# One level of Strassen's product in a decoder layer's up projection, with up and down as separate stages

## The chip, the cores and the metric

The kernel runs on one core of one Trainium2 chip. The metric is the device time of one execution in microseconds (us); the kernel before was run three times and the median counts. The engines are TensorE (PE; PEld is its weight load), VectorE (DVE), ScalarE (ACT), GpSimd (POOL) and SyncE (SP, which here only issues DMAs).

## The reference, cut to what matters

One layer of a hybrid decoder: an input projection, a group of attention heads beside a group of gated DeltaNet heads, an output projection, then an MLP, a gated per-layer embedding and a last norm. Sequence length and model width are 1024, the hidden width of the MLP is 4096, everything is float32. The change lies in the MLP:

```python
m = rmsnorm(h, norm_mlp[i])
h = h + jnp.square(jax.nn.relu(m @ w_up[i])) @ w_down[i]
```

## The kernel before

The residual stream is kept transposed, 128 channels by 1024 tokens in each of 8 tiles, in two halves of 512 tokens; `hT(hb, j)` (L989) is tile j of half hb. Every large product is made in three passes: `split` (L210) cuts a float32 operand into a high part (a cast on ScalarE, L211) and a low part (a subtraction on VectorE or GpSimd, L212), and `mm3` (L224) issues high x high, high x low and low x high into one PSUM bank. All matmuls go through one helper, so in the profile they have the line L95.

The weights come in blocks of 128 rows by 512 columns: `wunit` (L214) and `wunit2` (L270) load a raw block through SP into the pool `wraw` (two buffers) and split it into a buffer of `wsp` (four buffers), or, for the down projection, of `wdn` (six buffers).

The MLP: `norm_M` (L1189) scales the residual by the norm's gain and cuts it into high and low parts, 8 tiles for each half of the tokens, into M (the first half) and R1 (the second). `rows_M` (L1197) sums the squares over the channels and makes the row of reciprocal roots `rB`, by which results are multiplied after the product. Then a loop over 8 blocks of 512 hidden columns (L1257): two times (mp) an up unit of 256 columns, 8 contraction tiles x 2 column tiles x 2 halves x 3 passes = 96 matmuls into four banks; then `relu2` (L1239) evicts each bank on VectorE (maximum with zero, times `rB`, L1244), squares it on ScalarE (L1245) and splits it into `aT`. The 512 new hidden rows are used at once: the down product of the block (2 x 2 groups of 4 banks, 4 contraction tiles, 192 matmuls) is added to the residual on VectorE (L1295). Up units and down groups use four banks each in turn.

After the MLP comes the gate stage (from L1298): 16 gate weight blocks are split into M and R1, and for each of 8 token tiles the residual is transposed, multiplied and written out.

The order of the instructions on each engine is not that of the text: the framework's scheduler plans it with a simulated clock from the dependencies, the buffers that are free and the priority (the order of the text, or an earlier one under `ahead(mark)`, L266). On the chip each engine then follows its planned list.

Of the kernel before, what the change touches and what calls it, by code (L numbers as in the profile page):

```python
# [18 lines left out]
P = 128  # L19
# [92 lines left out]
def hybrid_block(ctx, tc, t, out):  # L112
# [111 lines left out]
    def mm3(o, lh, rh, first, last):  # L224
        for i, (a, b) in enumerate(PASSES):
            T.matmul(o, lh(a), rh(b), start=first and i == 0, stop=last and i == 2)
# [951 lines left out]

    px = ExitStack()
    mt0p = px.enter_context(tc.tile_pool(name="mt0p", bufs=1))  # L1180
    atp2 = px.enter_context(tc.tile_pool(name="atp2", bufs=1))
    wdn = px.enter_context(tc.tile_pool(name="wdn", bufs=6))
    M = [mt0p.tile([P, 8192], F32R, tag="M0", name="M0"), R1]
    aT = atp2.tile([P, 2, 4, S], F32R, tag="aT", name="aT")
    rB = [rsb[1]]

    FIRST = (4, 5, 0, 1, 2, 3, 6, 7)

    def norm_M(hb):  # L1189

        for j in FIRST:
            h, g = hT(hb, j), gmlp[:, j:j + 1]
            A.activation(uview(M[hb], 0, j), h, AF.Copy, scale=g)
            V.scalar_tensor_tensor(uview(M[hb], 1, j), h, g, uview(M[hb], 0, j).bitcast(F32),
                                   op0=ALU.mult, op1=ALU.subtract)

    def rows_M(hb):  # L1197
        for j in range(KT):
            x = cvp.tile([P, HB], F32, tag="cv", name=nm("sq")) if j else rB[hb]
            A.activation(x, hT(hb, j), AF.Square)  # L1200
            if j:
                V.tensor_tensor(rB[hb], rB[hb], x, op=ALU.add)
        yield
# [5 lines left out]
        yield  # L1209
        b, dg = bank(ps["w"]), row_bc(r, aT[:, :, 3, HB:])  # L1210
        yield
# [8 lines left out]
    psum(px, y=4, w=1)  # L1220
    zr, hn = part("Z"), part("AT0")
    rB.append(zr[:, 0:HB])
    with ahead(mark):
        norm_M(0)
        for _ in rows_M(0):
            pass
    norm_M(1)

# [10 lines left out]
    def relu2(b, m, hb):  # L1239
        if m % 2:  # L1240
            r = cvp.tile([P, 512], F32, tag="cv", name=nm("r"))
        else:
            r = zr[:, D + 512 * hb:D + 512 * hb + 512]
        V.scalar_tensor_tensor(r, b, 0.0, rB[hb], op0=ALU.max, op1=ALU.mult)  # L1244
        A.activation(r, r, AF.Square)  # L1245
        hi = aT[:, 0, m, hb * HB:(hb + 1) * HB]
        lo = aT[:, 1, m, hb * HB:(hb + 1) * HB]
        split(hi, lo, r, G)

    def late(bs):  # L1250

        yield from rows_M(1)
        for m in range(2):
            relu2(bs[m], m, 1)
        yield

    for c in range(FF // 512):  # L1257
        for mp in range(2):
            bs = quad() if c else banks(("wyyy", "gggy")[mp])
            order = range(KT // 2) if c + mp else [k // 2 for k in FIRST[::2]]  # L1260
            for i, k2 in enumerate(order):
                w = wunit2(t["w_up"], k2, c * 512 + mp * 256, G if k2 % 2 else V)
                if not c and mp:
                    for _ in range((0, 1, 2, 3).count(i)):
                        next(steps, None)
                for kk in range(2):
                    kt = k2 * 2 + kk
                    for hb in range(2):
                        for m in range(2):
                            o = kk * 256 + m * P  # L1270
                            mm3(bs[hb * 2 + m], lambda a: w[:, a, o:o + P],
                                lambda b: uview(M[hb], b, kt), i + kk == 0, i * 2 + kk == KT - 1)
            if c + mp == 0:
                rows_M(1)
            for hb in range(2):
                if c + mp == 0 and hb:
                    steps = late(bs[2:])
                    continue
                for m in range(2):
                    relu2(bs[hb * 2 + m], mp * 2 + m, hb)  # L1280
        for nh in range(2):
            wd = []
            for hb in range(2):
                bs = quad()
                for kt in range(4):
                    if hb == 0:
                        wd.append(wunit(t["w_down"][c * 512 + kt * P:c * 512 + (kt + 1) * P,
                                                    nh * 512:(nh + 1) * 512],
                                        sp=wdn, lo_eng=G if kt % 2 else V))
                    for m in range(4):  # L1290
                        mm3(bs[m], lambda a: wd[kt][:, a, m * P:(m + 1) * P],
                            lambda b: aT[:, b, kt, hb * HB:(hb + 1) * HB], kt == 0, kt == 3)
# [6 lines left out]
    for kt in range(KT):  # L1299
        for nh in range(2):  # L1300
            i = kt * 2 + nh
            o = (i % 8) * 1024
            m = M[i // 8]
# [12 lines left out]
    aTf = aT.rearrange("p b m s -> p (b m s)")  # L1316

    for tt in range(NT):

        nT = aTf[:, (tt % 4) * 2048:(tt % 4 + 1) * 2048].rearrange("p (b k s) -> p b k s", b=2, k=KT)  # L1320
# [115 lines left out]
```

## Time and profile before

| | |
|---|---|
| median of 3 runs | 1414.74 us (1413.67 to 1417.92) |
| profiled execution | 1413.97 us, span 1412.2 us |
| mean granted TensorE clock | 0.987 |
| the MLP's matmuls | from 579.0 to 1285.0 us of the span |
| instructions | 20118 |
| DMA traffic | 90.31 MB |

The span reaches from the first to the last instruction. A group of instructions is shown with its busy time and the mean of one; an engine's idle time is put down to what ended it. Matmuls overlap each other, so the spacing of their starts is their price, not the length of one.

### The profile page before, as it was taken

How to read it: one execution, taken by the hardware profiler on the slowest of the kernel's cores; microseconds unless marked ns; L12 is line 12 of the kernel's file. 1: busy time of each engine (PE TensorE's matmuls, PEld its weight loads, DVE VectorE, ACT ScalarE, POOL GpSimd, SP SyncE). 2: the span in 40 equal slices, each digit the busy share in tenths (PEclk: the TensorE clock that was granted, in tenths of full speed). 3: DMA queues.
4: the chain of work that ended last, by engine and by line, in shares of the span. 5: the costliest groups of instructions: out<-in, count | busy, mean ns of one | idle time of the engine just before them, and what ended most of it. 6: DMA issues, size and time to landing. Idle time of an engine off the chain costs nothing.

```text
span 1412.2 us, 20118 instructions
## 1 busy us (share of the span) xinstructions
PE 1369.5 (97%) x7760; PEld 1160.4 (82%) x7760; DVE 702.5 (50%) x1446; ACT 493.9 (35%) x1013; POOL 490.5 (35%) x492
## 2 busy tenths in 40 slices
PE   9989999899997999999999999999999999999997
PEld 7788778788887899888888888888888888888886
DVE  6776967998579965443121231212313223255333
ACT  7455465444343344351220312203122031344222
POOL 6673636531555343241320413204132041321222
PEclk9999999999999999999999999999999999999999
DMA  6312222223123222211210112101121011241101
GB/s 217 90 46 77 60 53 65 65 68 76 44 84 116 63 87 75 76 52 45 67 45 30 53 46 68 45 30 52 45 68 45 30 53 45 81 135 38 46 30 45
DMA packets 81200, 90.31 MB, mean 64 GB/s; under 512 B 15600, under 2 KB 63264, under 8 KB 81104
## 3 DMA queue, kind: packets, MB, share of 16 engines
q1 hardware_dynamic: 78208, 83.27, 19.9%
q10 hardware_dynamic: 2544, 4.99, 1.1%
q8 instruction: 61, 1.00, 0.3%
q0 software_dynamic: 352, 0.76, 0.2%
q14 instruction: 35, 0.29, 0.1%
HBM read 83.73 MB, written 5.26 MB: 63 GB/s over the span
## 4 chain that ended last, share of the span: by engine, by line
PE 78%; DVE 13%; DMA 3%; issue 2%; ACT 2%; POOL 1%; SPq 1%; POOLq 0%; DVEq 0%; ACTq 0%
PE bk L95 76%; DVE tp L771 2%; PE bk L99 2%; DVE cv L404 2%; DVE XS L772 1%; DMA AT<-in_xT 1%; DVE w L212 1%; POOL rsb L350 1%; DVE s L541 1%; DVE s L550 1%; DMA raw<-in_w_in 1%; DVE et L772 1%; DVE H L404 0%; ACT w L211 0%; DVE ka L741 0%
## 5 line engine op out<-in xcount | busy, mean ns | idle before, releaser
L95 PE MATMUL bk<-R,w 128*128 128x256 f32 (+1 forms) x1920 | 359.6, 334 | 4.4 <-DVE H L1014 3.0
L212 POOL TENSOR_TENSOR w<-raw,w 128x512 fp32r<-128x512 f32 x140 | 188.4, 1348 | 486.2 <-ACT w L211 382.6
L95 PE MATMUL bk<-aT,w 128*128 128x512 f32 x1536 | 349.8, 389 | 0.0
L211 ACT CAST w<-raw 128x512 fp32r<-128x512 f32 (+1 forms) x244 | 151.2, 620 | 554.5 <-PE bk L95 370.1
L95 PEld LDWEIGHTS bk<-aT,w 128*128 128x128 f32 x1536 | 288.3, 188 | 60.3
L95 PEld LDWEIGHTS bk<-R,w 128*128 128x128 f32 x1920 | 290.9, 192 | 46.9 <-issue 6.9
L212 DVE TENSOR_TENSOR w<-raw,w 128x512 fp32r<-128x512 f32 (+1 forms) x104 | 78.7, 757 | 248.4 <-ACT w L211 248.3
L95 PE MATMUL bk<-M,w 128*128 128x512 f32 x768 | 198.9, 394 | 0.0
L95 PEld LDWEIGHTS bk<-M,w 128*128 128x128 f32 x768 | 144.3, 188 | 34.5
L1295 DVE TENSOR_TENSOR H<-bk,H 128x512 f32<-128x512 f32 x96 | 64.8, 689 | 103.7 <-PE bk L95 103.7
L212 POOL TENSOR_TENSOR aT<-Z,aT 128x512 fp32r<-128x512 f32 x32 | 41.5, 1298 | 137.2 <-ACT aT L211 137.2
L95 PE MATMUL bk<-U,w 128*128 128x512 f32 (+1 forms) x384 | 76.3, 345 | 1.6 <-ACT ba L464 1.1
L95 PEld LDWEIGHTS bk<-U,w 128*128 128x128 f32 x384 | 58.4, 188 | 18.0 <-issue 7.3
L95 PE MATMUL bk<-w,R 128*128 128x256 f32 (+1 forms) x480 | 70.3, 298 | 0.1
L95 PE MATMUL bk<-w,U 128*128 128x256 f32 (+2 forms) x384 | 65.9, 326 | 3.4 <-ACT AT L470 1.6
L95 PEld LDWEIGHTS bk<-w,R 128*128 128x128 f32 x480 | 63.7, 200 | 2.5 <-issue 1.9
L95 PEld LDWEIGHTS bk<-w,U 128*128 128x128 f32 x384 | 57.2, 198 | 10.0 <-ACT AT L470 1.8
L1295 DVE TENSOR_TENSOR AT<-bk,AT 128x512 f32<-128x512 f32 x32 | 21.8, 690 | 57.0 <-PE bk L95 57.0
L547 ACT ACTIVATE s<-s,mx 128x257 f32<-128x257 f32 (+1 forms) x64 | 31.2, 490 | 50.8 <-DVE mx L545 46.4
L95 PE MATMUL bk<-R,aT 128*128 128x512 f32 (+1 forms) x204 | 47.8, 383 | 0.0
L95 PE MATMUL bk<-M,aT 128*128 128x512 f32 (+1 forms) x204 | 47.0, 378 | 0.0
L212 POOL TENSOR_TENSOR aT<-r,aT 128x512 fp32r<-128x512 f32 x32 | 45.2, 1413 | 0.2 <-ACT aT L211 0.2
(338 smaller groups left out, 1780.8 us busy)
## 6 DMA issues: line engine op xcount, KB each, us to landing
raw<-in_w_in SPq DMA_DIRECT2D x72, 256.0 KB, 2.8
raw<-in_w_up SPq DMA_DIRECT2D x64, 256.0 KB, 2.7
raw<-in_w_down SPq DMA_DIRECT2D x64, 256.0 KB, 2.9
raw<-in_w_o SPq DMA_DIRECT2D x32, 256.0 KB, 3.0
rawg<-in_w_gate SPq DMA_DIRECT2D x16, 256.0 KB, 2.9
AT<-in_xT SPq DMA_DIRECT2D x14, 256.0 KB, 3.9
out<-AT SPq DMA_DIRECT2D x7, 512.0 KB, 2.6
H<-in_xT ACTq DMA_DIRECT2D x3, 1024.0 KB, 5.1
```

The lines of the kernel that those rows point to most:

```text
L95: self.tc.nc.tensor.matmul(o, lh, rh, **k)
L99: self.tc.nc.tensor.transpose(o, x, i)
L211: A.copy(hi, src)
L212: lo_eng.tensor_tensor(lo, src, hi.bitcast(F32), op=ALU.subtract)
L350: eng.tensor_tensor(acc, acc, xr, op=ALU.add)
L404: V.scalar_tensor_tensor(cv if i < 3 else x[:, 3:], x[:, i:i + HB], cw[:, j, i:i + 1], cv, op0=ALU.mult, op1=ALU.add)
L541: V.tensor_tensor_reduce(out=s[:, i, lo:256], in0=b[:, i, lo:256], in1=amask[:, lo:256], scale=1.0, scalar=NEG, op0=ALU.add, op1=ALU.max, ...
L547: A.activation(s[:, i, lo:257], s[:, i, lo:257], AF.Exp, bias=mx[:, i:i + 1], accum_out=sm[:, i:i + 1])
L550: V.tensor_tensor(s[:, :, lo:256], s[:, :, lo:256], bc(sm, 2, 256 - lo), op=ALU.mult)
L771: V.tensor_tensor(tp, bc(LS[:, j, j + 1:32], 1, m), bc(X3[:, 0:m, j], 2, n), op=ALU.mult)
L772: V.tensor_tensor(X3[:, 0:m, j + 1:32], X3[:, 0:m, j + 1:32], tp, op=ALU.subtract)
L1295: V.tensor_tensor(h, bs[m], h, op=ALU.add)
```

## The change

The up projection is done in 16 units of 256 hidden columns. In each the weights (1024 x 256) and the activations are seen as 2 x 2 blocks: the contraction's 8 tiles are cut into even and odd ones, the hidden columns into two times 128, the tokens into two halves. Strassen's product, in Winograd's form, makes the four result blocks from 7 products instead of 8. The sums of activation blocks are made once, before the loop (`first_half`, `second_half`), and kept as seven operands X[1] to X[7], each split into high and low; X1, X2, X6 and X7 lie in the eight buffers of a new pool `mt`, X5 and X3 in R1, X4 in two parts that the output projection uses before. The sums of weight blocks are made on VectorE for each unit. `product` makes one of the seven products: 4 contraction tiles x 3 passes; products 2, 7 and 3 are accumulated onto the banks of products 1, 6 and 5, after these have been read. A unit uses four banks, the next unit the other four. The weights of products 4 and 3 share one buffer (`we`). The four result blocks are evicted (`put`), squared, and written to DRAM (`AD`, 16 tiles of 1 MB) through SP.

The first two units run product 1 of both, product 2 of both, and then the rest. After all 16 units a new loop makes the down projection: per block it loads four tiles of 128 x 1024 from `AD`, splits them into buffers of `mt`, and multiplies as before. The first block comes in half tiles through `wraw`, and its first four weights use `wsp` instead of `wdn`. `wdn` has five buffers and is opened when the up stage's pool `uw` is closed. The gate weights and token tiles of the last stage use R1 and `mt`.

```diff
-    def mm3(o, lh, rh, first, last):
+    def mm3(o, lh, rh, first, last, **k):
...
+    mt = px.enter_context(tc.tile_pool(name="mt", bufs=8))
+    ux = ExitStack()
+    uw = ux.enter_context(tc.tile_pool(name="uw", bufs=1))
+    AD = [dram.tile([P, 2048], F32, tag=f"AD{n}", name=f"AD{n}") for n in range(16)]
...
+    def tmp(i, n=HB):
+        p, tag, w = ((cvp, "cv", HB), (wraw, "raw", WN), (uw, "o", HB))[i]
+        return p.tile([P, w], F32, tag=tag, name=nm("t"), bufs=3 if i == 2 else None)[:, :n]
...
+    def first_half(i):
+
+        for p, j in ((1, 2 * i), (2, 2 * i + 1)):
+            h, g, (hi, lo) = hT(0, j), gmlp[:, j:j + 1], (cols(x, i) for x in X[p])
+            A.activation(hi, h, AF.Copy, scale=g)
+            V.scalar_tensor_tensor(lo, h, g, hi.bitcast(F32), op0=ALU.mult, op1=ALU.subtract)
+
+    def second_half(i):
+
+        j, k = 2 * i, 2 * i + 1
+        gj, gk = gmlp[:, j:j + 1], gmlp[:, k:k + 1]
+        t1, t2, t3, t4 = tmp(0), tmp(1), tmp(2), tmp(2)
+        G.tensor_tensor(t1, hT(1, j), hT(0, j), op=ALU.subtract)
+        A.activation(t1, t1, AF.Copy, scale=gj)
+        A.activation(t3, hT(1, j), AF.Copy, scale=gj)
+        V.scalar_tensor_tensor(t2, hT(1, k), gk, t1, op0=ALU.mult, op1=ALU.subtract)
+        V.scalar_tensor_tensor(t3, hT(1, k), gk, t3, op0=ALU.mult, op1=ALU.subtract)
+        V.scalar_tensor_tensor(t4, hT(0, k), gk, t2, op0=ALU.mult, op1=ALU.subtract)
+        for p, t, e in ((6, t2, V), (7, t3, G), (5, t1, G), (4, t4, V)):
+            hi, lo = (cols(x, i) for x in X[p])
+            split(hi, lo, t, e)
+        hi, lo = (cols(x, i) for x in X[3])
+        A.activation(hi, hT(1, k), AF.Copy, scale=gk)
+        V.scalar_tensor_tensor(lo, hT(1, k), gk, hi.bitcast(F32), op0=ALU.mult, op1=ALU.subtract)
+
+    class Quad:
+
+        def __init__(self, n):
...
+            raw = uw.tile([P, 8, 256], F32, tag="raw8", name=nm("raw8"), bufs=2)
+            for i in range(2):
+                SY.dma_start(raw[:, 4 * i:4 * i + 4],
+                             t["w_up"].rearrange("(k p) n -> p k n", p=P)[:, 4 * i:4 * i + 4, n * 256:n * 256 + 256])
+            r = raw.rearrange("p (i j) (f c) -> p j f i c", j=2, f=2)
+            self.A11, self.A12, self.A21, self.A22 = r[:, 0, 0], r[:, 1, 0], r[:, 0, 1], r[:, 1, 1]
+            self.S1, self.S2 = (uw.tile([P, 4, P], F32, tag=x, name=nm(x)) for x in ("S1", "S2"))
+
+        def product(self, p, b, src, eng):
+            first = p in (1, 6, 5, 4)
+            if first:
+                self.b[b] = bank(ps[("yyyy", "gggw")[self.n % 2][b]])
+            w = wsp.tile([P, 2, WN], F32R, tag="w", name=nm("w")) if p in (1, 6, 2, 7, 5) else \
+                uw.tile([P, 2, HB], F32R, tag="we", name=nm("w"))
+            w = w[:, :, :HB].rearrange("p b (i c) -> p b i c", i=4)
+            split(w[:, 0], w[:, 1], src, eng)
+            for i in range(4):
+                mm3(self.b[b], lambda a: w[:, a, i], lambda b: cols(X[p][b], i), first and i == 0, i == 3,
+                    skip_group_check=not first)
+
+        def put(self, r, f, hb, src=None):
+
+            V.scalar_tensor_tensor(r, r if src is None else src, 0.0, rB[hb], op0=ALU.max, op1=ALU.mult)
+            A.activation(r, r, AF.Square)
+            o = f * 1024 + hb * HB
+            SY.dma_start(AD[self.n][:, o:o + HB], r)
+
+        def p1(self):
+            self.product(1, 0, self.A11, V)
+            self.s = tmp(0)
+            A.copy(self.s, self.b[0])
+
+        def p6(self):
+            V.tensor_tensor(self.S1, self.A21, self.A22, op=ALU.add)
+            V.tensor_tensor(self.S2, self.S1, self.A11, op=ALU.subtract)
+            self.product(6, 1, self.S2, V)
+            self.U2 = tmp(2)
+            V.tensor_tensor(self.U2, self.b[1], self.s, op=ALU.add)
+
+        def p2(self):
+            self.product(2, 0, self.A12, G)
+            self.put(tmp(1), 0, 0, self.b[0])
+
+        def rest(self):
+            b, U2 = self.b, self.U2
+            V.tensor_tensor(self.A21, self.A11, self.A21, op=ALU.subtract)
+            self.product(7, 1, self.A21, V)
+            U3 = tmp(2)
+            V.tensor_tensor(U3, b[1], self.s, op=ALU.add)
+            self.product(5, 2, self.S1, V)
+            r = tmp(1)
+            V.tensor_tensor(r, b[2], U3, op=ALU.add)
+            self.put(r, 1, 1)
+            self.product(4, 3, self.A22, G)
+            V.tensor_tensor(U3, b[3], U3, op=ALU.add)
+            self.put(U3, 1, 0)
+            V.tensor_tensor(self.A12, self.A12, self.S2, op=ALU.subtract)
+            self.product(3, 2, self.A12, V)
+            V.tensor_tensor(U2, b[2], U2, op=ALU.add)
+            self.put(U2, 0, 1)
+
+    X[1], X[2], X[6], X[7] = ([mpart(), mpart()] for _ in range(4))
+    with ahead(mark):
+        for i in range(4):
+            first_half(i)
+        rows_M(0, V)
+    X[5] = [R1[:, 2048:4096], R1[:, 6144:8192]]
+    X[3] = [R1[:, 0:2048], R1[:, 4096:6144]]
+    X[4] = [part("AT0", F32R), part("Z", F32R)]
+    qs = [Quad(0), Quad(1)]
+    for i in range(4):
+        second_half(i)
+    for q in qs:
+        q.p1()
+    for q in qs:
+        q.p2()
+    rows_M(1, G)
+    for q in qs:
+        q.p6()
+        q.rest()
+    for n in range(2, 16):
+        q = Quad(n)
+        q.p1()
+        q.p6()
+        q.p2()
+        q.rest()
+    ux.close()
+    wdn = px.enter_context(tc.tile_pool(name="wdn", bufs=5))
...
     for c in range(FF // 512):
...
+        aT = []
+        for f in range(4):
+            a = mpart()
+            raw = wdn.tile([P, S], F32, tag="ra", name=nm("ra"), bufs=2) if c else None
+            for x in range(1 if c else 2):
+                o = slice(0, S) if c else slice(x * HB, x * HB + HB)
+                r = raw if c else wraw.tile([P, WN], F32, tag="raw", name=nm("ra"))[:, :HB]
+                SY.dma_start(r, AD[2 * c + f // 2][:, f % 2 * S + o.start:f % 2 * S + o.stop])
+                split(a[:, o], a[:, S + o.start:S + o.stop], r, G if f % 2 else V)
+            aT.append(a)
         for nh in range(2):
...
-                                        sp=wdn, lo_eng=G if kt % 2 else V))
+                                        sp=wdn if c + nh else None, lo_eng=G if kt % 2 else V))
```

In `rows_M` the additions of the second half move from VectorE to GpSimd.

## Rows read from the trace of the kernel before

**Rows 1.** The page's part 1: busy time, share of the span, instructions.
```profile
PE 1369.5 (97%) x7760; PEld 1160.4 (82%) x7760; DVE 702.5 (50%) x1446; ACT 493.9 (35%) x1013; POOL 490.5 (35%) x492
```
**Rows 2.** The page's part 4: the chain that ended last, by engine and line.
```profile
PE bk L95 76%; DVE tp L771 2%; PE bk L99 2%; DVE cv L404 2%; DVE XS L772 1%; DMA AT<-in_xT 1%; DVE w L212 1%; POOL rsb L350 1%; DVE s L541 1%; DVE s L550 1%; DMA raw<-in_w_in 1%; DVE et L772 1%; DVE H L404 0%; ACT w L211 0%; DVE ka L741 0%
```
**Rows 3.** Windows: length; busy (count) of PE, PEld, DVE, ACT, POOL; clock, DMA, GB/s.
```profile
579.01:1285.04 706.03, 706.03 (x3085) 578.07 (x3083) 201.91 (x290) 171.66 (x297) 172.68 (x132) 1.00 0.18 55
668.48:712.99 44.51, 44.51 (x193) 36.07 (x192) 8.99 (x14) 11.30 (x20) 11.89 (x9) 1.00 0.19 60
712.99:756.56 43.57, 43.57 (x193) 36.04 (x192) 12.99 (x20) 7.10 (x13) 8.93 (x7) 1.00 0.12 36
```
**Rows 4.** Timeline of PE: start, length, instructions of a down block.
```profile
712.99 43.73 PE L95 MATMUL bk<-aT,w 128*128 128x512 f32 x192
```
**Rows 5.** Timeline of PE in the gate stage: three groups of 12 matmuls.
```profile
1304.42 2.91 PE L95 MATMUL bk<-M,aT 128*128 128x512 f32 x12
1307.17 2.98 PE L95 MATMUL bk<-R,aT 128*128 128x512 f32 x12
1309.98 2.92 PE L95 MATMUL bk<-M,aT 128*128 128x512 f32 x12
```
**Rows 6.** Groups of instructions by form: busy us, mean ns, idle before.
```profile
L212 DVE TENSOR_TENSOR w<-raw,w 128x512 fp32r<-128x512 f32 x96 | 72.7, 757 | 244.8 <-ACT w L211 244.6
L1295 DVE TENSOR_TENSOR H<-bk,H 128x512 f32<-128x512 f32 x96 | 64.8, 689 | 103.7 <-PE bk L95 103.7
L1244 DVE SCALAR_TENSOR_TENSOR Z<-bk,rsb 128x512 f32<-128x512 f32 x16 | 11.1, 691 | 67.0 <-PE bk L95 67.0
L1194 DVE SCALAR_TENSOR_TENSOR M<-H,gmlp,M 128x512 fp32r<-128x512 f32 x8 | 5.4, 742 | 0.0
L211 ACT CAST w<-raw 128x512 fp32r<-128x512 f32 x236 | 146.2, 620 | 552.3 <-PE bk L95 370.1 <-DMA raw<-in_w_down 82.8 <-DMA raw<-in_w_up 52.4
L1193 ACT ACTIVATE M<-H,gmlp 128x512 fp32r<-128x512 f32 x8 | 5.0, 711 | 0.0
L212 POOL TENSOR_TENSOR w<-raw,w 128x512 fp32r<-128x512 f32 x140 | 188.4, 1348 | 486.2 <-ACT w L211 382.6 <-issue 81.4 <-DMA raw<-in_w_proj 14.1
```
**Rows 7.** Timeline of ACT (first row) and DVE around an up unit's end.
```profile
689.31 0.62 ACT L211 CAST w<-raw 128x512 fp32r<-128x512 f32 x1 [3.32 <-DMA raw<-in_w_down]
...
688.86 0.69 DVE L1244 SCALAR_TENSOR_TENSOR Z<-bk,rsb 128x512 f32<-128x512 f32 x1 [2.15 <-PE bk L95]
...
690.24 0.68 DVE L212 TENSOR_TENSOR w<-raw,w 128x512 fp32r<-128x512 f32 x1
690.84 0.68 DVE L1244 SCALAR_TENSOR_TENSOR Z<-bk,Z 128x512 f32<-128x512 f32 x1
```
**Rows 8.** Timeline of PE where the gate stage begins.
```profile
1286.88 1.09 PE L95 MATMUL bk<-M,aT 128*128 128x512 f32 x4
1287.81 0.60 PE L99 MATMUL bk<-con,H 128*128 128x128 f32 x4
1289.05 1.67 PE L95 MATMUL bk<-w,pw 128*128 128x512 f32 x6 [0.65 <-DVE AT L1295]
```
**Rows 9.** Before the first up matmul: a window (columns of rows 3), DVE, PE.
```profile
552.00:579.00 27.00, 26.35 (x219) 25.95 (x218) 19.39 (x31) 14.66 (x27) 11.89 (x9) 1.00 0.29 91
...
578.50 1.40 DVE L1014 TENSOR_TENSOR AT<-bk,AT 128x512 f32<-128x512 f32 x2 [0.87 <-PE bk L95]
...
578.77 0.40 PE L95 MATMUL bk<-AT,w 128*128 128x256 f32 x2
```
**Rows 10.** Timeline of the SP queue: eight loads of down weights.
```profile
686.74 20.20 SPq L217 DMA_DIRECT2D raw<-in_w_down  x8
```
**Rows 11.** The page's part 2 (40 slices) and DMA issues: KB each, us to landing.
```profile
GB/s 217 90 46 77 60 53 65 65 68 76 44 84 116 63 87 75 76 52 45 67 45 30 53 46 68 45 30 52 45 68 45 30 53 45 81 135 38 46 30 45
...
out<-AT SPq DMA_DIRECT2D x7, 512.0 KB, 2.6
...
H<-in_xT ACTq DMA_DIRECT2D x3, 1024.0 KB, 5.1
```

More of the change, by code (lines that the diff above doesn't have):

```diff
@@ L222, in hybrid_block @@
     PASSES = ((0, 0), (0, 1), (1, 0))
-    def mm3(o, lh, rh, first, last):
+    def mm3(o, lh, rh, first, last, **k):
         for i, (a, b) in enumerate(PASSES):
-            T.matmul(o, lh(a), rh(b), start=first and i == 0, stop=last and i == 2)
+            T.matmul(o, lh(a), rh(b), start=first and i == 0, stop=last and i == 2, **k)
     def mm3h(o, lh, rh, first, last):
@@ L1179, in hybrid_block, with mpart, rows_M @@
     px = ExitStack()
[L1180 to L1197, printed above, removed]
+    mt = px.enter_context(tc.tile_pool(name="mt", bufs=8))
+    ux = ExitStack()
+    uw = ux.enter_context(tc.tile_pool(name="uw", bufs=1))
+    rB = [rsb[1], uw.tile([P, HB], F32, tag="rB", name="rB1")]
+    AD = [dram.tile([P, 2048], F32, tag=f"AD{n}", name=f"AD{n}") for n in range(16)]
+    def mpart():
+        return mt.tile([P, 2048], F32R, tag="T", name=nm("T"))
+    def tmp(i, n=HB):
+        p, tag, w = ((cvp, "cv", HB), (wraw, "raw", WN), (uw, "o", HB))[i]
+        return p.tile([P, w], F32, tag=tag, name=nm("t"), bufs=3 if i == 2 else None)[:, :n]
+    def rows_M(hb, eng):
         for j in range(KT):
-            x = cvp.tile([P, HB], F32, tag="cv", name=nm("sq")) if j else rB[hb]
+            x = tmp(hb) if j else rB[hb]
             A.activation(x, hT(hb, j), AF.Square)
             if j:
-                V.tensor_tensor(rB[hb], rB[hb], x, op=ALU.add)
-        yield
+                eng.tensor_tensor(rB[hb], rB[hb], x, op=ALU.add)
         b, r = bank(ps["w"]), rstd[:, hb * 4:hb * 4 + 4]
@@ L1208, in rows_M @@
         G.tensor_tensor(r, r, mhalf[:, 0:4], op=ALU.pow)
-        yield
-        b, dg = bank(ps["w"]), row_bc(r, aT[:, :, 3, HB:])
-        yield
+        b, dg = bank(ps["w"]), row_bc(r)
         for i in range(2):
@@ L1220, in hybrid_block, with cols @@
     psum(px, y=4, w=1)
-    zr, hn = part("Z"), part("AT0")
[L1222 to L1227, printed above, removed]
+    def cols(x, i):
+        return x[:, i * HB:(i + 1) * HB]
+    X = {}
+    def first_half(i):
[3 more added lines that the diff above has]
+            V.scalar_tensor_tensor(lo, h, g, hi.bitcast(F32), op0=ALU.mult, op1=ALU.subtract)
@@ L1237, in quad @@
         return banks("gggw" if par[0] else "yyyy")
[L1239 to L1255, printed above, removed]
-    for c in range(FF // 512):
[L1258 to L1280, printed above, removed]
+    for c in range(FF // 512):
+        aT = []
[8 more added lines that the diff above has]
+            aT.append(a)
         for nh in range(2):
@@ L1301, in hybrid_block @@
             i = kt * 2 + nh
-            o = (i % 8) * 1024
-            m = M[i // 8]
+            if i > 7 and i % 2 == 0:
+                wg = mpart()
+            m, o = (R1, i * 1024) if i < 8 else (wg, i % 2 * 1024)
             raw = wdn.tile([P, 512], F32, tag="rawg", name=nm("rawg"), bufs=2)
```

7 lines of the change are left out of this document (4 added, 3 removed).

## The prediction

> **What bounds the kernel now.** I read the busy times first: the tensor engine's matmuls cover 97% of the span, VectorE 50%, ScalarE and GpSimd 35% each [rows 1]. The chain of waits says the same: 76% of it lies on the one line that issues matmuls [rows 2]. Then the stretch of the change, from the first up matmul to the last down matmul: 706.03 us in which PE is busy throughout, at a granted clock of 1.00 (the 2.4 GHz level), with VectorE busy 202 us, ScalarE 172 and GpSimd 173 [rows 3]. One up block of 192 matmuls lasts 44.51 us there, and the down block of 192 that begins where it ends lasts 43.57 [rows 3, 4]. So a matmul of 512 columns costs 0.2318 us in an up block and 0.2269 in a down block; the same shape goes 12 in 2.75 or 2.81 us in the gate stage (0.2292, 0.2343), by which tiles it reads [rows 5]. The listed 0.39 us of one matmul is longer because neighbours overlap; only the spacing counts. Fewer matmuls shorten this stretch, as long as the other engines feed PE without gaps.
>
> **The sum.** It is made against the profiled execution, 1413.97 us (span 1412.2, 1.77 around it), 0.8 below the median of the runs, 1414.74.
>
> Products. Before: 8 blocks x 192 = 1536 up matmuls. After: 16 units of 256 hidden columns, each 7 products x 4 contraction tiles x 3 passes = 84, together 1344. The 192 removed are worth 192 x 0.2318 = 44.5 us. If the new tiles (other buffers, other addresses) run at 0.2269, the up stage takes 304.9 instead of 356.1, a gain of 51.2; at 0.2343 it takes 314.9, a gain of 41.2. I take 44.5, because these are still weights from the same pool against wide activation tiles.
>
> Inside a unit PE needs 84 x 0.2318 = 19.5 us. VectorE gets 4 sums of weight blocks and 5 low parts at 0.757, 5 sums out of PSUM at 0.689 and 4 evictions at 0.691: 6.8 + 3.4 + 2.8 = 13.0 us. ScalarE gets 7 casts, a copy and 4 squares, taken at a cast's 0.620: 7.4. GpSimd gets 2 low parts at 1.348: 2.7 [rows 6]. All fit, VectorE at two thirds. What decides is order. A product needs its bank read (the copy after product 1, the sums after 6, 7 and 5), but another product of 12 x 0.2318 = 2.8 us always lies between, and a read takes 0.7. Its weights need only the raw block and a weight buffer, so they can be made early if the planner of the instruction order puts them in front of evictions that wait for PE. It does so now: the high and low part of a down weight, whose matmuls start 22 us later, stand between the evictions of an earlier up unit [rows 7], although the text has them far behind. Price of the remaining hand-offs: 0 to 16 x 2.8 = 45 us, the upper end a whole product's time per unit; nearest are the present up blocks with no idle time at all, so I take 2.
>
> Products 4 and 3 share a single weight buffer, so product 3's weights can be split only after product 4's last matmul: 0.62 + 0.757 plus two hand-offs, about 1.6 us. Uncovered that is 16 x 1.6 = 26 us. The cover is the next unit's product 1, in other banks with its weights in other buffers. PE's order is not fixed by the text: at the gate stage 4 gate matmuls were put before transposes and products that come earlier in the text but were still waiting for VectorE [rows 8]. I take 2 us (the last unit, which has nothing to cover it, and small misses), and keep 0 and 26 as ends.
>
> Entry. The second half's preparation replaces 8 scalings by, per pair of tiles, 7 ScalarE instructions (four splits at 0.620, three scalings at 0.711: 4.6 us), 6 of VectorE (4 at 0.742, 2 at 0.757: 4.5 us) and 3 of GpSimd (4.0 us) [rows 6]. Four pairs make 18.5, 17.9 and 16.2 us, and GpSimd also takes the 7 row sums (9.4) that VectorE did. From 552 to 579 ScalarE has 12.3 us free, VectorE 7.6, GpSimd 15.1 [rows 9], and most of the 8 removed scalings of each of the first two (5.7 and 5.9 us) fall away there. The last pair waits for the output projection's last sums at 578.50, and the part for product 4 for the tiles that its last matmuls read until 579 [rows 9]. Cover is the 4 products that need only the first half, 48 x 0.2318 = 11.1 us. Upper bound: all of GpSimd's 25.6 us begin at 579, 14.5 exposed; lower bound 0. Three pairs need 13.9, 13.4 and 12.1 us, about the room before 579, so I take 2.
>
> Handover from up to down. The down stage is new work: 4 activation loads and splits per block. The first block takes them as 8 half loads plus 4 weight loads through the two raw buffers, which two results of the last unit use too. In the present trace such loads pass those buffers 8 in 20.2 us, 2.5 each [rows 10]. Their target tiles come free from product 1 of the last unit on, 72 x 0.2318 = 16.7 us before its end. If the first weight comes behind 8 halves and 2 results, it is the 11th load, 27.5 us, so 11 us of PE idle; if it is moved ahead, 0. After that a load per 2.5 us keeps up with 2.8 us per contraction tile. I take 5.
>
> Down blocks. A part of 1024 columns is charged as two of 512. ScalarE gets 4 x 1.24 + 8 x 0.62 = 9.9 us; GpSimd 4 x 1.348 + 2 x 2.70 = 10.8; VectorE 4 x 0.757 + 2 x 1.51 + 16 x 0.689 = 17.1, all under 43.57 [rows 3, 6]. Traffic is 4 MB per block, 96 GB/s; the page's first slice moved 217 [rows 11]. Stores of 512 KB land in 2.6 us and loads of 1 MB in 5.1 [rows 11], and a result is read back hundreds of us after it was stored. SP's queue carries both: a store waiting for its square holds the next unit's raw load behind it, but that has one whole unit, 19.5 us, to arrive. Cost 0; without that cover 5.1 us per unit. The tail gets more room (8 rotating tiles): 0, at most the 0.65 us of idle that PE now has there [rows 8].
>
> Sum: 1413.97 - 44.5 + 2 + 2 + 2 + 5 = 1380.5.
>
> **One rule weighed.** The trace shows each waiting eviction at the head of VectorE with 2.15 us idle before it [rows 7]: what stands behind it waits too. The Trainium skill, TensorE: Matmul & The Clock Gate, in its table of specifications, says that VectorE's, ScalarE's and GpSimd's queues are strict first-in first-out. The trace agrees as far as this wait shows. By the row that a planned order can put weights ahead of such waits the sum stays as above; by the rule with a plan that doesn't, it is the first rival's below.
>
> **The rivals.**
> - VectorE holds the weights (slower). If evictions stand ahead of the next product's block sum and low part, PE waits 0.691 + 0.757 + 0.757 = 2.2 us at a product. Per unit this can happen before products 7, 5, 4 and 3; at two of them it is 16 x 2 x 2.2 = 70 us: 1380.5 - 2 + 70 = about 1449. Break-even is 35.5 / 16 = 2.2 us, one such wait per unit. For it: VectorE rises to two thirds, with five reads per unit that release PE. Against it: rows 7.
> - The single buffer is not covered: 1380.5 - 2 + 26 = about 1405. For it: 16 equal places with a buffer short; the same trouble comes if PE's planned order has product 3 a little too early. Against it: rows 8. The Trainium skill, Perfetto Trace Analysis, section Optimization Strategy, says that a bubble that repeats can mean too few buffers; no run so far shows such a bubble in this stage.
> - Everything hides and the new tiles run at 0.2269: 1413.97 - 51.2 = about 1363.
> - No gain: the entry's and the handover's upper ends (14.5 and 11) with half the single buffer's price (13) and the 2 for hand-offs give back 40.5: about 1410. Against it: PE has no idle time at 579 now, with the present preparation [rows 3].
>
> **How the numbers follow.** Forecast 0.62 (own range 1369 to 1393), single buffer 0.17, VectorE 0.10, full gain 0.06, no gain 0.05. About 4.2 us, 0.3%, is what a measurement can tell from no change. Faster: forecast, full gain, and nearly all of the buffer's case, 0.85; same 0.05; slower 0.10. The range runs from 1364, near the full gain, to 1406, the buffer's case; left out are VectorE, no gain and a few outer cases, under 0.2.
>
> **What would show it.** Right: some 1344 up matmuls in about 315 us, PE without repeated idle, next unit's product 1 among product 3's; idle of a few us at the first down matmul. Wrong: PE idle before product 3 released by a low part or cast, 16 times; PE idle before product 7 or 5 released by VectorE; several us of idle about 11 us after the first up matmul; clock below 1.00 in the up stage; or a down block longer than 43.6 us.

## The result, and the profile after

**Slower, by about 1%.** The changed kernel takes 1428.96 us (median of 4 runs, 1427.18 to 1430.78), the kernel before 1415.02 beside it (4 runs): ratio 1.0096, 95% interval 1.0075 to 1.0117. The forecast was 1380.5, range 1364 to 1406. The profiled run took 1428.09 us, span 1426.3, which is 14.1 longer than the span before.

The page of the changed kernel, busy times, clock and chain by engine and line:

```profile
PE 1338.7 (94%) x7568; PEld 1132.3 (79%) x7568; DVE 879.4 (62%) x1665; ACT 540.1 (38%) x1069; POOL 481.2 (34%) x465
...
PEclk9999999999999999779999999969999999999999
...
PE bk L95 69%; DVE tp L771 2%; PE bk L99 2%; DVE cv L404 2%; DVE XS L772 1%; DMA ra<-AD 1%; DMA AT<-in_xT 1%; DVE w L212 1%; DMA raw<-in_w_up 1%; POOL rsb L350 1%; DVE s L541 1%; DVE s L550 1%; POOL rB L1200 1%; DVE et L772 1%; DMA raw<-in_w_in 0%
```

Against [rows 1, 2]: matmuls fell from 97% of the span to 94%, VectorE rose from 50% to 62%, and the share of the chain on the matmuls' line fell from 76% to 69%. The clock line has two dents, in slices 17 and 18 and in slice 27; a slice is 35.7 us, so they are at 571 to 642 and 927 to 963. That is the entry into the up stage and the handover to the down stage. Windows cut at these places (columns: busy us and instructions of PE, weight loads, VectorE, ScalarE, GpSimd; granted clock; DMA share; GB/s):

```profile
552.00:585.15 33.15, 29.64 (x224) 29.22 (x222) 28.88 (x33) 20.26 (x36) 22.47 (x16) 0.90 0.32 101
585.15:628.15 43.00, 23.18 (x76) 17.74 (x77) 27.65 (x36) 18.91 (x33) 22.31 (x16) 0.68 0.03 13
628.15:923.16 295.01, 294.72 (x1269) 237.74 (x1267) 186.52 (x268) 101.77 (x177) 43.59 (x29) 1.00 0.31 104
923.16:956.68 33.52, 13.61 (x38) 9.71 (x37) 15.98 (x16) 14.00 (x22) 8.57 (x6) 0.64 0.74 229
956.68:1299.00 342.32, 342.32 (x1508) 283.20 (x1509) 136.67 (x188) 77.28 (x112) 77.72 (x49) 1.00 0.31 97
```

The first up matmul starts at 585.15 instead of 579.01 [rows 3]: 6.1 late. The 43.00 us behind it hold 64 matmuls of the products (the other 12 of the 76 recorded make the factor rows); at 0.2318 these need 14.8, so 28.2 are lost. The middle stretch is clean: 1269 matmuls in 295.01 us, 0.2325 each, 0.29 us idle. The handover holds 36 wide matmuls, 8.3 us of work in 33.52: 25.2 lost. From there on the down stage runs without idle time; its tail is 0.8 shorter than before. So -44.5 + 6.1 + 28.2 + 25.2 - 0.8 = +14.2, against 14.1 measured. **The saved matmuls are worth what was forecast; the two transitions, 43 and 34 us long, and the late start give back 59.5.**

TensorE at the entry and at the handover, in order of time (us of the group behind its start; in brackets idle time before, and what ended it; the last row is cut where the view ends, at 1000):

```profile
574.56 1.86 PE L95 MATMUL bk<-ones,rsb 128*128 128x1 f32 x8 [2.48 <-DVE AT L1014]
...
585.15 1.25 PE L95 MATMUL bk<-T,w 128*128 128x512 f32 x4 [1.03 <-ACT w L211]
588.88 0.77 PE L95 MATMUL bk<-dg,ones 128*128 128x512 f32 x1 [2.48 <-DVE dg L372]
592.14 7.74 PE L95 MATMUL bk<-T,w 128*128 128x512 f32 x20 [2.50 <-DVE w L212]
599.94 5.73 PE L95 MATMUL bk<-T,w 128*128 128x512 f32 x24
618.41 1.87 PE L95 MATMUL bk<-ones,rB 128*128 128x1 f32 x8 [12.75 <-POOL rB L1200]
622.38 1.22 PE L95 MATMUL bk<-T,w 128*128 128x512 f32 x2 [2.10 <-ACT w L211]
...
924.24 0.74 PE L95 MATMUL bk<-R,w 128*128 128x512 f32 x2 [0.93 <-ACT w L211]
925.90 4.14 PE L95 MATMUL bk<-R,w 128*128 128x512 f32 x10 [0.93 <-DVE w L212]
947.36 8.58 PE L95 MATMUL bk<-T,w 128*128 128x512 f32 x24 [17.32 <-ACT w L211]
956.68 43.58 PE L95 MATMUL bk<-T,w 128*128 128x512 f32 x189 [0.74 <-ACT w L211]
```

Between 585.15 and 628.15 the stops sum to 19.8 us. The rest of the 28.2 is the factor rows' matmuls and the clock: 20 matmuls take 7.74 us behind the stops (0.387 each) and 24 take 5.73 a little later (0.239). The largest stop belongs to no product: PE waits for the eight small matmuls that close the row sums of the second half, `rB`, and product 6 of the first unit stands behind them on PE's list. Who made them late, on GpSimd and ScalarE:

```profile
609.04 9.32 POOL L1200 TENSOR_TENSOR rB<-rB,t 128x512 f32<-128x512 f32 x7 [5.04 <-ACT t L1198]
```

```profile
608.33 0.63 ACT L1198 ACTIVATE t<-H 128x512 f32<-128x512 f32 x1 [1.21 <-DMA AD<-t]
...
621.61 0.19 ACT L211 CAST rh<-rstd 128x4 fp32r<-128x4 f32 x1 [5.27 <-POOL rstd L1205]
```

The squares need temporary tiles that product 2's results hold until they are stored (608.33, released by the store). Then seven sums take 9.32 us on GpSimd, the matmuls follow at 618.41, the root at 620, and ScalarE, which has waited 5.27 us for that root, has the next weights' casts queued behind `rh`.

At the handover, SyncE's queue (columns: start, us over the group, issue, count):

```profile
898.52 18.20 SPq L1278 DMA_DIRECT2D AD<-t  x6
918.76 0.32 SPq L1360 DMA_DIRECT2D ra<-AD  x1
922.73 0.32 SPq L1278 DMA_DIRECT2D AD<-t  x1
924.67 2.01 SPq L1360 DMA_DIRECT2D ra<-AD  x2
926.78 0.60 SPq L1278 DMA_DIRECT2D AD<-t  x1
930.19 2.18 SPq L1360 DMA_DIRECT2D ra<-AD  x2
933.25 0.32 SPq L1278 DMA_DIRECT2D AD<-t  x1
935.32 2.22 SPq L1360 DMA_DIRECT2D ra<-AD  x4
937.59 1.28 SPq L1388 DMA_DIRECT2D rawg<-in_w_gate  x2
940.33 0.33 SPq L1360 DMA_DIRECT2D ra<-AD  x1
944.10 0.33 SPq L217 DMA_DIRECT2D raw<-in_w_down  x1
```

The first of the eight half tiles stands behind six stores of results. The last of these stores, issued at 916.40, takes product 2's result out of a `raw` buffer, and the half waits 1.9 us more until that store has landed. The eight then go through the two `raw` buffers with more stores between them (two of the four loads from 935.32 on belong to the second block), and the first down weight is issued behind all of them, at 944.10, 25.3 us after the first half.

### The profile page after: what moved, and what is told of

It is laid out like the page before. It is cut to its first block, busy times and chain, and to the rows that moved or that the text cites. A ratio compares the mean times of both kernels' runs of the same rounds, so it can differ in the third digit from the quotient of the medians.

```text
span 1426.3 us, 20423 instructions
## 1 busy us (share of the span) xinstructions
PE 1338.7 (94%) x7568; PEld 1132.3 (79%) x7568; DVE 879.4 (62%) x1665; ACT 540.1 (38%) x1069; POOL 481.2 (34%) x465
## 4 chain that ended last, share of the span: by engine, by line
PE 71%; DVE 16%; DMA 5%; issue 3%; POOL 2%; ACT 2%; SPq 1%; DVEq 0%; POOLq 0%; ACTq 0%
PE bk L95 69%; DVE tp L771 2%; PE bk L99 2%; DVE cv L404 2%; DVE XS L772 1%; DMA ra<-AD 1%; DMA AT<-in_xT 1%; DVE w L212 1%; DMA raw<-in_w_up 1%; POOL rsb L350 1%; DVE s L541 1%; DVE s L550 1%; POOL rB L1200 1%; DVE et L772 1%; DMA raw<-in_w_in 0%
## 5 line engine op out<-in xcount | busy, mean ns | idle before, releaser
L95 PE MATMUL bk<-T,w 128*128 128x512 f32 x2304 | 542.9, 394 | 24.0 <-ACT w L211 21.5
L95 PEld LDWEIGHTS bk<-T,w 128*128 128x128 f32 x2304 | 436.3, 190 | 121.7 <-ACT w L211 23.3
L95 PE MATMUL bk<-R,w 128*128 128x256 f32 (+1 forms) x1536 | 259.3, 320 | 6.2 <-DVE H L1014 3.0
L95 PEld LDWEIGHTS bk<-R,w 128*128 128x128 f32 x1536 | 220.1, 194 | 34.4 <-issue 6.9
L1276 ACT ACTIVATE t<-t 128x512 f32<-128x512 f32 x64 | 40.3, 632 | 99.1 <-DVE t L1275 99.1
L95 PE MATMUL bk<-AT,w 128*128 128x256 f32 (+1 forms) x256 | 65.5, 346 | 0.0
L212 POOL TENSOR_TENSOR T<-ra,T 128x1024 fp32r<-128x1024 f32 (+1 forms) x18 | 39.5, 2198 | 73.1 <-ACT T L211 73.1
L212 DVE TENSOR_TENSOR T<-ra,T 128x1024 fp32r<-128x1024 f32 (+1 forms) x18 | 21.7, 1204 | 46.0 <-ACT T L211 42.5
L95 PEld LDWEIGHTS bk<-AT,w 128*128 128x128 f32 x256 | 44.0, 198 | 5.6
L95 PE MATMUL bk<-R,T 128*128 128x512 f32 (+1 forms) x204 | 48.2, 383 | 0.0
```

The source lines that it names most:

```text
L95: self.tc.nc.tensor.matmul(o, lh, rh, **k)
L212: lo_eng.tensor_tensor(lo, src, hi.bitcast(F32), op=ALU.subtract)
```

## The experiments

Each was run once unless a ratio is given. The kernel before took 1418.1 us beside the first four, 1412.89 beside the next four, 1414.1 beside the three after those; so a few us between groups mean nothing by themselves, and there the rows decide. The changed kernel was not run again in these groups: what is said to be below it is below its profiled run of 1428.09 us and is uncertain by as much.

**e1_no_sums.** The second half's row sums are left out, its factor row is the first half's.

```diff
-    rows_M(1, G)
+    rB[1] = rB[0]
```

> Leaves out the row sums of the second half of the tokens (its squares, GpSimd's 7 sums, the small matmuls), and uses the first half's factors for both halves. Theory A (PE stands behind the row sums: 12.75 us idle at 618.41 and 2.10 at 622.38, with the small matmuls about 16 us between the last product 2 and the first product 6): about 1412 us, 16 less than the changed kernel's 1428.1, and product 6 follows product 2 within 1 us. Rival B (product 6's own operands, made by the three engines in second_half, are what is late): at most 4 us gained, 1424 or more.

1407.24 us, 20.9 below the profiled run of the changed kernel: theory A, with 5 us more than it expected. TensorE at its entry:

```profile
588.30 0.77 PE L95 MATMUL bk<-dg,ones 128*128 128x512 f32 x1 [2.47 <-DVE dg L372]
591.56 6.46 PE L95 MATMUL bk<-T,w 128*128 128x512 f32 x20 [2.49 <-DVE w L212]
...
598.09 8.55 PE L95 MATMUL bk<-T,w 128*128 128x512 f32 x36
606.48 0.63 PE L95 MATMUL bk<-R,w 128*128 128x512 f32 x2
```

The stops up to 592 stay, those of 12.75 and 2.10 are gone: the first matmuls that read the tiles `R` come at 606.48 instead of 624.25, 17.8 earlier, with ten more product matmuls done by then. The sums are more than half of the loss at the entry, and when they are left out nothing else there takes their place.

**e3_staged.** The first down block's activations come by two loads of 1 MB into the buffers of the up weights, before that pool is closed; the `raw` buffers are left to the weights.

```diff
+    stage = []
+    for x in range(2):
+        r8 = uw.tile([P, 8, 256], F32, tag="raw8", name=nm("raw8"), bufs=2).rearrange("p k n -> p (k n)")
+        SY.dma_start(r8, AD[x])
+        stage.append(r8)
+    aT0 = []
+    for f in range(4):
+        a = mpart()
+        split(a[:, :S], a[:, S:], stage[f // 2][:, f % 2 * S:f % 2 * S + S], G if f % 2 else V)
+        aT0.append(a)
...
+            if c == 0:
+                aT.append(aT0[f])
+                continue
```

> The first down block's activations come by two loads of 1 MB through the up stage's raw8 buffers, which have no further unit to serve, instead of 8 half loads through the two raw buffers; the raw buffers are left to the down weights. Theory A (9 loads one after the other through two buffers, some 3 us each, hold the first down weight): the 17.32 us and the three shorter stops at the handover shrink to under 8 us, about 1405 to 1411 us. Rival B (the target tiles come free too late, or SP's queue with stores waiting for their squares is what holds the loads): less than 6 us gained, 1422 or more.

1408.85 us, 19.2 below: theory A. The only stop that is left at its handover:

```profile
927.52 6.01 PE L95 MATMUL bk<-T,w 128*128 128x512 f32 x18 [2.92 <-ACT w L211]
```

So the handover's loss is the eight halves in front of the weights, not the amount of data: the same 2 MB in another place cost 2.92 us of stop instead of 17.32 and its neighbours.

**e4_vector_only.** The 12 GpSimd instructions of the second half's preparation go to VectorE.

```diff
-        G.tensor_tensor(t1, hT(1, j), hT(0, j), op=ALU.subtract)
+        V.tensor_tensor(t1, hT(1, j), hT(0, j), op=ALU.subtract)
...
-        for p, t, e in ((6, t2, V), (7, t3, G), (5, t1, G), (4, t4, V)):
+        for p, t, e in ((6, t2, V), (7, t3, V), (5, t1, V), (4, t4, V)):
```

> The 12 GpSimd instructions of second_half go to VectorE. Theory A (VectorE's instructions of 0.7 us take 1.78 while GpSimd works on the same memory; 13 of them lose 1.05 us each, 13.6 us in all, against 12 x 0.68 = 8.2 us of added work): the slow ones return to 0.7, first up matmul earlier, 1420 to 1427 us. Rival B (VectorE has simply too much to do at the entry): 1432 to 1437 us.

1427.46 us, just above theory A's range and below rival B's: no change in time, but not for want of an effect. VectorE's instructions from 566 to 606, grouped by shape (count, busy us, mean ns, idle before), in the changed kernel:

```profile
L1239 DVE SCALAR_TENSOR_TENSOR t<-H,gmlp,t 128x512 f32<-128x512 f32 x4 | 6.0, 1512 | 0.0
...
L1014 DVE TENSOR_TENSOR AT<-bk,AT 128x512 f32<-128x512 f32 x4 | 2.6, 676 | 0.0
```

and in this one:

```profile
L1239 DVE SCALAR_TENSOR_TENSOR t<-H,gmlp,t 128x512 f32<-128x512 f32 x4 | 3.0, 741 | 0.0
```

The windows of these 40 us, first of the kernel before, then of the changed kernel, then of this one:

```profile
566.00:606.00 40.00, 40.00 (x227) 34.81 (x226) 17.23 (x25) 16.23 (x29) 11.20 (x9) 1.00 0.24 73
```

```profile
566.00:606.00 40.00, 31.18 (x155) 26.56 (x153) 39.60 (x43) 21.81 (x38) 27.64 (x18) 0.79 0.03 8
```

```profile
566.00:606.00 40.00, 28.36 (x163) 23.94 (x161) 37.51 (x56) 23.68 (x42) 9.41 (x7) 0.87 0.07 25
```

VectorE, busy for 17.23 us there in the kernel before, does 56 instructions in 37.51 us of work where it did 43 in 39.60 in the changed kernel, since those that GpSimd's work had lengthened shrink back. The first stop fell from 2.48 to 0.65 us, and the granted clock from 552 to 579 was 1.00. But the first up matmul comes only 0.7 earlier, at 584.48, behind a stop of 4.33 for its weights, and the row sums still came last (the stop before their small matmuls is 13.49).

**e5_roots_late.** The sums stay on GpSimd where they were; their small matmuls, the root and the factor row come behind product 5 of the first unit.

```diff
+        yield
         b, r = bank(ps["w"]), rstd[:, hb * 4:hb * 4 + 4]
...
             self.product(5, 2, self.S1, V)
+            for _ in tail:
+                pass
...
-    rows_M(1, G)
+    tail = rows_M(1, G)
+    next(tail)
```

> The row sums stay, but what follows them (the small matmuls, the root, the row of factors) comes in the text behind product 5 of the first unit instead of ahead of product 6. Theory A (only the planned place on PE's list costs; the sums themselves fit beside products 6, 7 and 5): 1410 to 1416 us. Rival B (ScalarE's squares and the raw buffers that they share with the stored results hold product 6's weights as well): 1420 to 1428 us.

1419.14 us, 9.0 below, between the two expectations. Product 6 now follows without a stop (36 matmuls from 598.19, then the first that read `R` at 606.54), but the sums' time comes back further on:

```profile
619.22 4.57 PE L95 MATMUL bk<-R,w 128*128 128x512 f32 x12 [4.20 <-DVE t L1307]
...
627.61 1.22 PE L95 MATMUL bk<-T,w 128*128 128x512 f32 x2 [3.04 <-ACT w L211]
```

VectorE and ScalarE stop behind the same sums and the same root that PE stood behind before. Moving the consumer is worth 9.0 of the 20.9 us that leaving out the sums gave.

**d1_dg_own_buffer.** `dg` takes the idle buffer `we`, not a slot of the weight pool.

```diff
-        b, dg = bank(ps["w"]), row_bc(r)
+        b, dg = bank(ps["w"]), row_bc(r, uw.tile([P, 2, HB], F32R, tag="we", name=nm("dg")))
```

> The changed kernel, but the factor rows dg of the two halves are built in the buffer `we` (idle until product 4) instead of a slot of the weight pool. Between the first up matmul (585.15) and 592.14 the changed kernel has three stops of 1.03, 2.48 and 2.50 us, and its matmuls there are paced by VectorE's weight work. Theory A (the weight pool is short there: dg holds a slot that product 1's or 2's weights need): the three stops shrink by 2 to 5 us in all, 1423 to 1426 us against 1428. Theory B (VectorE is simply behind with its queue until about 590): nothing changes, 1427 to 1429.

1424.0 us, inside theory A's numbers but on a chip where the kernel before took 2.1 us less than in the comparison of the result; by the time alone this decides nothing. Its rows hold something of both theories: the stops between 585 and 592 are gone, 24 matmuls run without one from 582.84 on (A), and then there are stops of 1.96, 1.27, 1.96, 2.14, 1.22 and 2.46 us, by VectorE's or ScalarE's work (B). VectorE is busy for all 40 us from 566 to 606.

**c2_spread.** e3's staging; the row sums of the second half two tiles after each pair's preparation; their close behind product 5.

```diff
+            if hb and j and j % 2 == 0:
+                yield
...
+        yield
...
+    tail = rows_M(1, G)
     for i in range(4):
         second_half(i)
+        next(tail)
...
-    rows_M(1, G)
     for q in qs:
         q.p6()
-        q.rest()
+        q.rest(tail)
```

> Three edits together: the first down block's activations through two 1 MB loads in their own buffers; the row sums of the second half spread, two tiles after each pair's preparation, instead of all behind the fourth pair; their small matmuls, root and factor row behind product 5 of the first unit. Alone, the first was worth 19.5 us and leaving the row sums out 21. Theory A (the 28 us at the entry are the row sums' place in the queues of GpSimd and ScalarE and on PE's list): the sums now end with the last pair, near 600, and no product waits for them; most of the 21 comes back, 1390 to 1398 us. Theory B (it is the amount of preparation on GpSimd, ScalarE and VectorE, wherever it stands): only the 9 us that the later place of the root alone was worth: 1398 to 1403.

1398.07 us, 30.0 below the changed kernel, where theory A's range ends and theory B's begins. The staging alone gave 19.2 (e3_staged) and the late close alone 9.0 (e5_roots_late), together 28.2: spreading the sums is not shown to add more than the 2 us that are left, which is what theory B says. No product waits for the sums, but VectorE's backlog is there still (from 584.08 to 604.27 it is busy without a gap); the largest stop at the entry is now this one:

```profile
603.17 0.80 PE L95 MATMUL bk<-T,w 128*128 128x512 f32 x1 [2.82 <-ACT T L211]
```

**c5_spread_dg** is c2_spread with the edit of d1_dg_own_buffer.

> As the spread kernel with staged activations, and with dg in the buffer `we`. If the weight pool is short at the first up matmuls, another 3 to 8 us below that kernel; if VectorE's backlog sets it, the same within 2 us.

1404.82 us, 6.8 slower than the kernel beside it; neither expectation. `we` is also the buffer of products 4 and 3, and the planned order changed with it: the small matmuls of `dg` now have 3.63 and 4.01 us of idle time before them, and the first stop at the handover grew from 3.32 to 6.29. As in d1_dg_own_buffer, 24 matmuls now follow the output projection without a stop (from 579.33), so `dg`'s slot in the weight pool, or the planned order that comes with it, did hold the first products; letting them go brings no time, since what follows waits for VectorE.

**c6_spread_dg_vector** is that kernel with e4's edit.

> As the last, with the GpSimd work of the second half's preparation and the row sums on VectorE (12 and 7 instructions of about 0.7 us, 13 us more on VectorE, 25 us off GpSimd). Theory A (GpSimd working beside VectorE makes VectorE's instructions longer, and GpSimd is the slower of the two): 2 to 8 us faster than the kernel beside it. Theory B (VectorE is the engine with the backlog at the entry, and more work on it only moves the wait): 3 to 10 us slower.

1402.61 us, 2.2 faster than c5_spread_dg. The expectation counts 19 instructions; the kernel moves the 12 of the preparation, and the seven row sums stay on GpSimd. The sign is theory A's, the size near the noise.

**e6_no_second_half.** Leaves out all of the second half's preparation and sums: products 6, 7, 5, 4 and 3 read the first half's tiles. With e3's staging. It also leaves four of the eight `mt` buffers free.

```diff
-    X[1], X[2], X[6], X[7] = ([mpart(), mpart()] for _ in range(4))
+    X[1], X[2] = ([mpart(), mpart()] for _ in range(2))
...
+    X[6] = X[5] = X[4] = X[1]
+    X[7] = X[3] = X[2]
     qs = [Quad(0), Quad(1)]
-    for i in range(4):
-        second_half(i)
+    rB[1] = rB[0]
...
-    rows_M(1, G)
```

> Leaves out the whole preparation of the second half's operands (the four second-half calls) and its row sums: products 6, 7, 5, 4 and 3 read the tiles of the first half, and the second half's factor row is the first's. With the first down block's activations staged as in e3_staged. Theory A (all of what the prediction missed lies in two places, the preparation at the entry and the loads at the handover, and the units themselves cost 0.2325 us per matmul as predicted): 1344 x 0.2318 and the down stage as they are, no more than 5 us at the entry and 5 at the handover, 1370 to 1379 us. Theory B (the units also lose by themselves at the start, through the planned order, the weights' buffers or the banks): still 10 us or more between the first up matmul and the steady stage, 1382 to 1392.

1373.64 us, theory A. Windows of this kernel before the first up matmul, and from there to its next stop, 4.10 us at the handover (columns as above):

```profile
552.00:580.32 28.32, 27.60 (x231) 27.30 (x230) 20.14 (x30) 11.57 (x23) 11.72 (x9) 1.00 0.38 121
580.32:892.31 311.99, 307.89 (x1334) 249.89 (x1332) 199.50 (x283) 111.68 (x193) 50.61 (x33) 1.00 0.32 109
```

The stretch is 311.99 us with that stop, 307.9 without it, for 1332 up matmuls (the last 12 come behind the stop, and 2 of the 1334 are the output projection's): 0.2311 each, between the 0.2269 and the 0.2318 of the forecast. Banks, buffers and the planned order of the units lose next to nothing: up to the handover there is no stop, and the first up matmul comes 1.3 us later than in the kernel before. Against e3_staged, which ran in another group, the span falls by 35.3; 6.1 + 28.2 = 34.3 was read from the windows above as the entry's loss.

**c4_vector** is c2_spread with e4's edit (again 12 instructions; the sums stay on GpSimd).

> The spread kernel with staged activations (c2_spread), the second half's GpSimd work and row sums moved to VectorE (19 instructions of 0.74 instead of 1.3 to 1.8 us). Theory A (at the entry VectorE and GpSimd lengthen each other's instructions, 0.74 to 1.78 and 1.27 to 1.72, so GpSimd's part is no relief): 2 to 6 us below c2_spread, 1392 to 1396. Theory B (the sum of VectorE's own work is what counts): 3 to 8 above, 1401 to 1406.

1392.77 us, 5.3 below c2_spread, which ran in another group: theory A. What made no difference while the row sums came last is worth some 5 us once they don't (2.2 between c5_spread_dg and c6_spread_dg_vector, which ran in one group).

**f1_spread_cv.** c2_spread, and the last unit's two results that used `raw` buffers go through `cv`.

```diff
-            self.put(tmp(1), 0, 0, self.b[0])
+            self.put(tmp(0 if self.n == 15 else 1), 0, 0, self.b[0])
...
-            r = tmp(1)
+            r = tmp(0 if self.n == 15 else 1)
```

> c2_spread, and the last unit's two results that go through the raw weight buffers go through the `cv` buffers instead. If the remaining 5 us at the handover of c2_spread (3.32 and 1.66 us idle before the first down weights) come from raw buffers that these results hold, 3 to 5 us less: 1393 to 1395. If the cv buffers, free only after the sums of products 6 and 7, hold the unit up instead, the same or 1 to 3 us more.

1390.93 us, 7.1 below c2_spread, more than the 3 to 5 expected. The one stop left at the handover:

```profile
917.97 2.60 PE L95 MATMUL bk<-R,w 128*128 128x512 f32 x10 [1.06 <-DVE w L212]
```

The stops account for 3.32 + 1.66 - 1.06 = 3.9 of it. The other 3 are the clock behind the stops, as the windows of the handover show, first of c2_spread, then of this kernel:

```profile
900.00:940.00 40.00, 35.02 (x136) 27.41 (x135) 19.43 (x23) 13.67 (x21) 13.22 (x8) 0.87 0.54 178
```

```profile
900.00:940.00 40.00, 38.94 (x168) 31.26 (x168) 25.57 (x28) 15.89 (x24) 15.21 (x8) 1.00 0.59 190
```

A matmul costs 35.02 / 136 = 0.258 us of busy time there in c2_spread, 0.232 here.

**f2_vector_cv** is f1_spread_cv with e4's edit.

> The edits that paid, together: activations of the first down block staged, row sums spread and their root late, the second half's preparation without GpSimd (c4_vector, 1392.8), the last unit's two results through the cv buffers (f1_spread_cv, 7.1 below c2_spread). If the two places are independent: 1392.8 - 7.1 = 1386, and no more than 3 us from it. If what f1_spread_cv gained was GpSimd's relief at the entry or spread between runs, 1390 to 1394. Either would be 1.5 to 2% below the kernel before.

1385.74 us (5 runs, 1384.45 to 1390.23) against 1413.02 (9 runs): ratio 0.9814, 95% interval 0.9796 to 0.9832. That is the 1386 expected if the two places are independent, and this version beats both kernels. Its windows, from the end of the output projection's matmuls to the first product without a stop, and from there to the end of the handover's stop of 0.99:

```profile
577.00:612.00 35.00, 23.50 (x90) 17.82 (x90) 34.97 (x47) 20.00 (x36) 16.05 (x9) 0.76 0.04 15
612.00:912.16 300.16, 299.17 (x1291) 242.07 (x1290) 197.42 (x279) 109.30 (x189) 53.13 (x34) 1.00 0.35 115
```

VectorE is busy for 34.97 of the 35.00 us: what is still lost at the entry is VectorE's time. That fits the 12.1 us which separate this kernel from e6_no_second_half, where the work is absent. Six of the 47 instructions still take 1.75 to 1.80 us, while GpSimd makes row sums and low parts of weights; taking the sums off GpSimd too was not tried.

## Why the prediction was wrong

**Products: right.** 192 matmuls x 0.2318 = 44.5. The units ran at 0.2325 per matmul over 1269 of them, and the full-gain rival's 0.2269 did not come.

**Order inside a unit and the single buffer: right, priced at 2 + 2, came to about 1.** 1269 x (0.2325 - 0.2318) is 0.9, with 0.29 us of idle time. The planner did put weights ahead of waiting evictions, and another unit's product between 4 and 3. The rival in which VectorE holds the weights and the one in which the buffer is not covered didn't occur: neither has its repeated stop.

**Entry: the step that failed first.** "Three pairs need 13.9, 13.4 and 12.1 us, about the room before 579, so I take 2", bounds 0 to 14.5; measured 34.3, more than twice the upper bound. Three things in it were wrong.
- It added each engine's instructions and let the three run side by side at the durations of the kernel before: 0.742 on VectorE, 1.348 on GpSimd [rows 6]. Here they lengthened each other, VectorE's to 1.512 in the mean, and VectorE, for which 7.6 us were free, fell behind. The output projection waited 2.48 us for a VectorE sum, ran on at a lower clock and ended some 5 us later than before; with the stop of 1.03 behind it the first up matmul was 6.1 late, and stops up to 592 followed. Taking GpSimd's part away (e4_vector_only) or `dg` out of the weight pool (d1_dg_own_buffer) moved these stops and did not end them; VectorE stayed busy nearly throughout.
- It counted the row sums as 9.4 us of GpSimd's time and didn't follow who reads them. Eight small matmuls on PE's list, a root, and a cast at the head of ScalarE's queue stand behind the sums, and product 6 and its weights behind those. Leaving the sums out gave 17.8 us at that place (e1_no_sums); closing them late gave 9.0 (e5_roots_late).
- It had no term for the clock: at the entry the granted clock is 0.68, and the matmuls behind the stops cost 0.387 instead of 0.23.

**Handover: the second.** "If the first weight comes behind 8 halves and 2 results, it is the 11th load, 27.5 us, so 11 us of PE idle; if it is moved ahead, 0 ... I take 5"; measured 25.2, more than twice the 11. (1.9 of it are two stops for the weights of the last unit's product 3, which the sum had under the single buffer.) The mechanism was the one named, at its bad end: the weight was issued 25.3 us after the first half. But the cover of 16.7 us was not there. The first half was issued at 918.76, behind six stores of results on SyncE's queue, when about 30 up matmuls were left, not 72. There the queue and the buffer held it together: the last of the six stores, of product 2's result, could not go before its square at 915.74, and the half's buffer was free when that store had landed. Taking the activations off those buffers gave back 19.2, and with the results off them too the stop fell to about 1 us.

**Down blocks, traffic and tail: right.** From 956.68 on 1508 matmuls take 342.32 us, 0.2270 each against 0.2269 in [rows 3, 4], without idle time; the tail is 0.8 shorter.

**The rivals.** "No gain" named the two places that decided, at 0.05, and stopped at the same upper bounds; the slower side was given to a repeated wait in the units, where the trace of before had evidence against it. The slower case that came was two waits that happen once each. Both bounds had been made by subtracting a cover that the sum took for granted.

With these two places relieved the rest of the forecast's sum stands: f2_vector_cv is 5.2 us above 1380.5, and e6_no_second_half, which leaves the preparation out, 6.9 below.

## What to carry to other kernels

A rewrite that saves work in a long steady stage can pay for it where the stage begins and ends: cost those transitions by following each new result to its reader on every queue, not by adding up engines' times. A reduction whose result is needed late still stands in front of whatever follows its small closing matmuls on PE's list; close it late (9.0 us here; that spreading its sums adds to this was not shown). Before counting a load as hidden, ask which buffer it lands in and what must leave that buffer first.

## What was not expected of the hardware

- VectorE and GpSimd lengthen each other's work. From 566 to 606 in the changed kernel, VectorE's `t<-H,gmlp,t` took 1.512 us in the mean, single ones 1.78, against 0.741 with GpSimd's part moved away; GpSimd's low parts took 1.60 to 1.64 in the mean, against 1.348 in [rows 6]. In the same stretch, VectorE's sums that read a PSUM bank and one SBUF tile kept 0.676. The Trainium skill, SBUF — State Buffer, section Who interferes with whom, says that a VectorE instruction with two SBUF inputs contends with a GpSimd instruction that reads SBUF, and that one with at most one SBUF input, outside the modes that use both ports, doesn't; the trace agrees, and the numbers above are its price here.
- Giving GpSimd's 12 instructions to VectorE cost VectorE no time in the same 40 us: 56 instructions in 37.51 us of work instead of 43 in 39.60.
- Short stops of PE cost more than themselves. With the stop of 2.48 us before 574.56, the stretch from 552 to 579 has a granted clock of 0.92 and 191 matmuls; with one of 0.65 at the same place (e4_vector_only) it has 1.00, the 2.4 GHz level throughout, and 223. Six small matmuls of the output projection take 1.28 us behind the longer stop, 0.71 behind the shorter one. At the entry and the handover, at 0.68 and 0.64, part of the loss that looks like busy PE is the lower level of 1.2 GHz.
